# Weights of an MoE and FFN kernel stored on the host in the order of the 1 MB loads, one 8 KB run per partition

## The chip, the cores and the metric

One core of one Trainium2 chip runs the whole program. The metric is the device time in microseconds (us) of one execution. The kernel before took 2174.83 us (median of three runs: 2169.98, 2174.83, 2175.6). The execution that the profiler recorded took 2171.46 us, with a span of 2169.7 us from its first to its last instruction.

## The reference, cut

Two blocks follow each other on 256 tokens of width 1024. Block 1 mixes (gated linear attention beside latent attention) and then runs a routed mixture of 64 experts, two per token. Block 2 has two layers, each a mixer between two dense gated FFNs of hidden width 2816. All arrays are float32.

```python
def hier_moe(u, wg, bg, we, be, w_gate, w_up, w_down):     # w_gate, w_up: 64 x 1024 x 512; w_down: 64 x 512 x 1024
    ...
    def expert_block(args):
        xb, e = args
        hdn = jax.nn.silu(xb @ w_gate[e]) * (xb @ w_up[e])
        return hdn @ w_down[e]
    ...

def swiglu(x, w_gate, w_up, w_down):                       # 1024 x 2816, 1024 x 2816, 2816 x 1024, four times
    return (jax.nn.silu(x @ w_gate) * (x @ w_up)) @ w_down
```

What is computed is the same before and after. The large arrays are these weights: 402.7 MB for the experts (64 of 6 MB), 138 MB for the four FFNs, and some 49 MB for the mixers of both blocks and the memory keys and values.

## The kernel before

All weights come from HBM once, in parts of at most 1 MB, each into one slot of 128 partitions by 2048 floats (8 KB per partition). `load` (L140) takes the next slot of a ring and issues one DMA on SyncE's queue; every weight load has that line. The ring has 17 slots in the expert stage (`a_done` makes it so: three of pool w1, two of w2, five of w4 and seven more) and 3 slots in block 2. A load waits until the last reader of its slot is done. SyncE issues in program order, so later loads wait behind it.

Which bytes of HBM a load takes is set by a rearranged view of the weight:

```python
v = i[src][e].rearrange("(t p q) n -> p t (q n)", p=P, q=2)     # expert gate, up: row 256 t + 2 p + q
v = i["expert_w_down"][e].rearrange("(k p) n -> p k n", p=P)    # expert down: row 128 k + p
v = w[:, c0:c0 + n].rearrange("(k p) n -> p k n", p=P)          # cols_w: 4 or 8 pieces of n columns
```

So one partition of a load is filled from several pieces of HBM. The 1 MB parts of an expert take two runs of 4 KB per partition, and all runs of one part together are 1 MB without a gap. The FFN's gate and up loads (`cols_w`) take four runs of 2 KB per partition, or eight of 1 KB for the first chunk of 256 columns, from rows that lie 11,264 bytes apart; its down loads (`rows_w`) take two of 4 KB. The four w_in chunks of block 1 take four runs of 1856 or 2048 bytes, the memory weights four of 2 KB, `mla_w_qb` two of 3 KB, and the second layer's mixer loads four of 1056 to 2048 bytes or eight of 1 KB.

The program has three stages. Block 1's mixer and router (`phase_a`, to about 180 us) load w_in, w_out and the first experts. The expert stage (`moe`) takes the experts in order. Per expert TensorE multiplies with gate (tile pg from eg) and up (pu from eu), transposes (pt), multiplies with down (pd from ed) and scatters the result back to the tokens (po); every eight experts it gathers the tokens of the next eight (ps). The loads of an expert are issued in the order gate, up, down, two parts each (`load_expert`). In block 2 (from about 1139 us, `ffn` and the mixers) each loaded part is split by ScalarE and VectorE into two halves of its precision (`split`, wh and wl), and TensorE makes three passes per part. `overflow` loads expert weights again where an expert has more than 32 tokens; no load of it is among the DMA issues of the profile.

Of the kernel before, what the change touches and what calls it, by code (L numbers as in the profile page):

```python
# [18 lines left out]
P = 128  # L19
D = 1024  # L20
KD = D // P
# [3 lines left out]
EPS = 1e-6  # L25
LN_EPS = 1e-5
ALL, UPPER, LOWER = (0, 1, 2), (0, 2), (1,)


def _consts():  # L30
# [58 lines left out]
class Kern:  # L89
# [48 lines left out]
    def load(self, shape, src, name, q=None, pool=None):  # L138
        t = self.slot(shape, name, pool=pool)
        (q or self.nc.sync).dma_start(t, src)  # L140
        return t
# [98 lines left out]
    def phase_a(self):  # L240
        nc, tc, i = self.nc, self.tc, self.i
        h = self.h
        w_in = i["w_in"]
# [11 lines left out]
            return sb.tile(shape, F32, tag="t2", bufs=6, name=name)  # L255

        def wcols(c0, n):
            return [self.load([P, 4, n], w_in[512 * u:512 * u + 512, c0:c0 + n].rearrange("(k p) n -> p k n", p=P), "win")
                    for u in range(2)]

        toks = ((0, NM), (NM, P), (NM + P, P))
        met = t4([NM, D], "met")
# [6 lines left out]
        for b in range(2):  # L269
            nc.sync.dma_start(h[:, b, :], i["x"][b * P:(b + 1) * P, :])  # L270
        nc.sync.dma_start(self.cst[0], i["cst0"])
        rest = wcols(0, 464)
        qk = wcols(464, 512)
        wa2 = sb.tile([P, 256], F32, name="wa2")
# [16 lines left out]
        for j in (2, 0, 1):  # L291
            src, n = blocks[j][:2]
# [12 lines left out]
        for j in (0, 2, 1):  # L305
            src, n, c0 = blocks[j]
            for g in range(2):
                p = self.ps()
# [22 lines left out]
        la, e = lae[:, 0], lae[:, 1]  # L331
# [283 lines left out]
        groups = (("kra", 384, 80, 0), ("kv", 256, 128, 0), ("l0", 0, 128, NM), ("l1", 128, 128, NM))  # L615
        zp = {g[0]: self.ps("z") for g in groups}
        rest = [self.split(t, u == 0) for u, t in enumerate(rest)]
        wqb = self.load([P, 2, 768], i["mla_w_qb"].rearrange("(k p) n -> p k n", p=P), "wqb")
        wkvb = self.load([P, 1024], i["mla_w_kvb"], "wkvb")
        for n, c0, w, t0 in groups:  # L620
            zpart(zp[n][:w, t0:NT], rest[0], 0, c0, w, t0, (0, 1))
# [50 lines left out]
        v = self.mp.tile([P, 4, 512], F32, tag="xs", name="v")  # L672
# [32 lines left out]
        for b in range(2):  # L705
            nc.scalar.activation(r_tile()[:, b, :], rp[b], AF.Silu)
        rdone.append(True)

        wo = [self.load([P, 2, D], i["w_out"][256 * u:256 * u + 256, :].rearrange("(k p) n -> p k n", p=P), "wo")
              for u in range(4)]  # L710
        ws = {}
        acc, done = [None, None], False
        for q, b in ((2, 0), (2, 1), (3, 0), (3, 1), (0, 0), (1, 0), (0, 1), (1, 1)):
# [173 lines left out]
    def load_expert(self, e):  # L887
        i = self.i
        out = []
        for n, src in (("eg", "expert_w_gate"), ("eu", "expert_w_up")):  # L890
            v = i[src][e].rearrange("(t p q) n -> p t (q n)", p=P, q=2)
            out.append([self.load([P, 2, D], v[:, 2 * u:2 * u + 2, :], n) for u in range(2)])
        v = i["expert_w_down"][e].rearrange("(k p) n -> p k n", p=P)
        out.append([self.load([P, 2, D], v[:, 2 * u:2 * u + 2, :], "ed") for u in range(2)])
        return out

    def gather(self, e0, parts=((0, 8),)):
# [83 lines left out]
    def overflow(self):  # L981

        nc, tc, i = self.nc, self.tc, self.i
        n = nc.values_load(self.over, min_val=0, max_val=512)
        h = self.h
        mp, mq = self.mp, self.mq
        u2T = mp.tile([P, KD, NX], F32, tag="xg", name="ou")
        wgu = mp.tile([P, 2, D], F32, tag="oh", name="owg")
        wg, wu = (wgu[:, q].rearrange("p (t q n) -> p t q n", t=4, q=2) for q in range(2))
        wd = mp.tile([P, 4 * NT], F32, tag="y", bufs=2, name="owd")[:, :D]  # L990
        s = mq.tile([P, NX], F32, tag="C", bufs=2, name="os")
        gc = mq.tile([P, 2], F32, name="ogc")
        with tc.If(n > 0):
            for b in range(2):
                xv = self.xs[:, b, :].rearrange("p (t x q) -> p t q x", q=2, x=P)
                for k in range(KD):
                    p = self.ps("ot")
                    self.T(p[:, :P], xv[:, k // 2, k % 2, :])
                    nc.vector.tensor_scalar_mul(u2T[:, k, b * P:b * P + P], p[:, :P], self.col("ffn")[:, k:k + 1])
            with tc.For_i(0, 64, 1) as e:  # L1000
                po = [[self.ps("fo") for _ in range(2)] for _ in range(2)]
                nc.sync.dma_start(gc, self.Gov[:, :, bass.ds(e, 1)].rearrange("p b o -> p (b o)"))
                for f in range(4):
                    fs = slice(f * P, f * P + P)
                    for t in range(4):
                        for dst, src in ((wg, "expert_w_gate"), (wu, "expert_w_up")):
                            nc.sync.dma_start(dst[:, t], i[src][bass.ds(e, 1), 256 * t:256 * t + 256, fs].rearrange(
                                "o (p q) n -> p (o q) n", q=2))
                    nc.sync.dma_start(wd, i["expert_w_down"][bass.ds(e, 1), fs, :].rearrange("o p n -> p (o n)"))
                    pp = []  # L1010
                    for wt in (wg, wu):
                        p = self.ps("fg")
                        for k in range(KD):
                            self.mm(p[:, :NX], wt[:, k // 2, k % 2, :], u2T[:, k, :], start=k == 0, stop=k == KD - 1)
                        pp.append(p)
                    nc.scalar.activation(s, pp[0][:, :NX], AF.Silu)
                    nc.vector.tensor_mul(s, s, pp[1][:, :NX])
                    for b in range(2):
                        for nh in range(2):
                            self.mm(po[b][nh], s[:, b * P:b * P + P], wd[:, nh * 512:nh * 512 + 512],  # L1020
                                    start=f == 0, stop=f == 3)
                for b in range(2):
                    for nh in range(2):
                        cs = slice(nh * 512, nh * 512 + 512)
                        nc.vector.scalar_tensor_tensor(h[:, b, cs], po[b][nh], gc[:, b:b + 1], h[:, b, cs],
                                                       ALU.mult, ALU.add)
# [16 lines left out]


    def kv_w(self, l):
        return self.i["w_kv_mem_2"][l].rearrange("(k p) n -> p k n", p=P)

    def load_kv(self, l):
        v = self.kv_w(l)
# [92 lines left out]
        self.mm(out, xh, wl, start=False, stop=False)  # L1142
        self.mm(out, xl, wh, start=False, stop=stop)

    def cols_w(self, w, c0, n):

        v = w[:, c0:c0 + n].rearrange("(k p) n -> p k n", p=P)
        kk = 8 if n <= 256 else 4
        return [lambda k0=k0: self.load([P, kk, n], v[:, k0:k0 + kk, :], "wc") for k0 in range(0, KD, kk)]

    def rows_w(self, w, r0, nk):

        v = w[r0:r0 + nk * P, :].rearrange("(k p) n -> p k n", p=P)
        return [lambda k0=k0: self.load([P, 2, D], v[:, k0:k0 + 2, :], "wr") for k0 in range(0, nk, 2)]

    def xw(self, b, out, w, k0, passes=ALL):

# [84 lines left out]
    def ffn(self, l, j, ln, nxt):  # L1242

        nc, i = self.nc, self.i
        last = nxt is None
        wg, wu, wd = (i[n][l, j] for n in ("ffn_w_gate_2", "ffn_w_up_2", "ffn_w_down_2"))
        g, bt = self.ln_params(l, ln)
        ctx = ExitStack()
        fp = ctx.enter_context(self.tc.tile_pool(name="fp", bufs=1))
        chunks = [(0, 256)] + [(256 + 512 * c, 512) for c in range(5)]  # L1250
        nch = len(chunks)
        nkt = sum(n for _, n in chunks) // P
        acc = [None, None]
# [63 lines left out]
        w = self.split(self.cols_w(wg, *chunks[1])[1]())  # L1317
        for b in range(2):
            gu(1, "g", 1, b, w)
        for c in range(1, nch):  # L1320
            if c > 1:
                for h, x in enumerate(self.cols_w(wg, *chunks[c])):
                    w = self.split(x())
                    for b in range(2):
                        gu(c, "g", h, b, w)
            for h, x in enumerate(self.cols_w(wu, *chunks[c])):
                w = self.split(x(), late=c == 1)
                for b in range(2):
                    gu(c, "u", h, b, w)
            c0, n = chunks[c - 1]  # L1330
            ws = self.rows_w(wd, c0, n // P)
            if c < nch - 1:
                for q, x in enumerate(ws):
                    w = self.split(x())
                    for b in range(2):
                        down(c - 1, q, b, w)
        c = nch - 1
        ws += self.rows_w(wd, chunks[c][0], 4)
        w = [None] * 4
# [491 lines left out]
    AT += _w  # L1831


def prep(inp):

    v = {k: np.asarray(x) for k, x in inp.items()}
    v = {k: x[0] if x.ndim > 2 and x.shape[0] == 1 else x for k, x in v.items()}
    rows = [v[k].reshape(4, P, 2).transpose(0, 2, 1) if k == "ffn_norm" else v[k] for _, k in ROWS]
    rows = np.concatenate([x.reshape(-1, P) for x in rows])
    d = {"cst0": CONSTS[0], "cst1": CONSTS[1], "rows": np.concatenate([rows, np.zeros((P - len(rows), P), rows.dtype)])}  # L1840
    w = v["w_in"]
    d["w_in"] = np.concatenate([w[:, 1552:], w[:, 1536:1552], w[:, :1536]], 1)
    w = v["mla_w_qb"].reshape(256, 4, 192)
    d["mla_w_qb"] = np.concatenate([w[:, :, :P].reshape(256, 512), w[:, :, P:].reshape(256, 256)], 1)
    d["wa2"] = np.zeros((P, 256), v["gla_w_a2"].dtype)
    d["wa2"][64:80], d["wa2"][96] = v["gla_w_a2"], v["gla_b_a"].reshape(-1)
    d["wr"] = np.concatenate([v["router_group_w"], v["router_expert_w"]], 1).reshape(4, P, 144).transpose(1, 0, 2)
    d["br"] = np.concatenate([v["router_group_b"].reshape(1, -1), v["router_expert_b"].reshape(1, -1)], 1)
    d["qk_conv_w_2"] = v["qk_conv_w_2"].reshape(64, 96)
    for k in ("mix_norm", "final_norm"):  # L1850
        d[k] = v[k].reshape(1, D)
    for k, x in v.items():
        if k not in d and not any(k in m for m in MIX) and k not in [m for _, m in ROWS]:
            d[k] = x
    return {k: np.ascontiguousarray(x) for k, x in d.items()}
# [14 lines left out]
```

## Time and profile before

| | us |
|---|---|
| three runs | 2169.98, 2174.83, 2175.6 |
| the profiled execution | 2171.46 |
| its span | 2169.7 |
| TensorE busy | 2003.4 (92% of the span) |
| expert stage, first to last matmul of pg, pu, pd | 178.9 to 1140.1 |
| block 2, from there to the end | about 1030 |
| SyncE's DMA queue: packets, bytes | 195,554, 602.55 MB |

A busy TensorE is not a TensorE at its peak, since matmuls are pipelined and their ends are modelled. The share of the DMA engines is the sum of the times of their packets over 16 engines and the stretch. It passes 100% where consecutive packets of one engine overlap a little, so a stretch with about 102% is one in which no engine rests. A packet here is one run of bytes in HBM that goes to one partition; each load adds 16 packets of 4 bytes (one per engine, which tell that it has landed).

### The profile page before, as it was taken

How to read it: one execution, taken by the hardware profiler on the slowest of the kernel's cores; microseconds unless marked ns; L12 is line 12 of the kernel's file. 1: busy time of each engine (PE TensorE's matmuls, PEld its weight loads, DVE VectorE, ACT ScalarE, POOL GpSimd, SP SyncE). 2: the span in 40 equal slices, each digit the busy share in tenths (PEclk: the TensorE clock that was granted, in tenths of full speed). 3: DMA queues.
4: the chain of work that ended last, by engine and by line, in shares of the span. 5: the costliest groups of instructions: out<-in, count | busy, mean ns of one | idle time of the engine just before them, and what ended most of it. 6: DMA issues, size and time to landing. Idle time of an engine off the chain costs nothing.

```text
span 2169.7 us, 36697 instructions
## 1 busy us (share of the span) xinstructions
PE 2003.4 (92%) x15959; PEld 1402.0 (65%) x15959; DVE 955.4 (44%) x1460; ACT 668.3 (31%) x885; POOL 31.3 (1%) x28
## 2 busy tenths in 40 slices
PE   8989888988889898988889999999999999999998
PEld 7767544534444354444447887888888887888886
DVE  6553322222222222222226555775447455887445
ACT  6423111111111111111114433544434432854332
POOL 3000000000000000000000000000000000000000
PEclk9979999999999999999999999999999999999999
DMA  6448999999999999999996654546555553445551
GB/s 225 175 178 348 411 388 411 413 412 413 411 413 412 412 412 413 411 408 412 408 379 219 229 179 144 204 140 219 185 177 192 181 188 92 163 156 186 183 179 74
DMA packets 195942, 604.96 MB, mean 279 GB/s; under 512 B 9889, under 2 KB 26529, under 8 KB 195778
## 3 DMA queue, kind: packets, MB, share of 16 engines
q1 hardware_dynamic: 195554, 602.55, 73.0%
q8 instruction: 127, 2.08, 0.4%
q14 instruction: 37, 0.30, 0.0%
q10 hardware_dynamic: 224, 0.03, 0.0%
HBM read 601.49 MB, written 1.05 MB: 278 GB/s over the span
## 4 chain that ended last, share of the span: by engine, by line
PE 58%; DMA 23%; DVE 4%; SPq 1%; ACT 1%; issue 1%; DVEq 0%; ACTq 0%
DMA ed<-in_expert_w_down 12%; PE fu L117 11%; PE fg L117 11%; PE fd L117 11%; DMA eu<-in_expert_w_up 10%; PE pd L117 5%; PE po L117 4%; PE cu L117 2%; PE mu L117 2%; PE ps L117 2%; PE pg L117 2%; PE pu L117 2%; PE mo L117 2%; SPq L140 1%; PE ht L114 1%
## 5 line engine op out<-in xcount | busy, mean ns | idle before, releaser
L976 DVE SCALAR_TENSOR_TENSOR h<-po,G,h 128x512 f32<-128x512 f32 x256 | 192.1, 751 | 359.0 <-PE po L117 338.7
L1123 DVE TENSOR_TENSOR wl<-wc,wh 128x2048 fp32r<-128x2048 f32 (+2 forms) x108 | 240.3, 2231 | 181.7 <-ACT wh L1117 181.5
L117 PE MATMUL pd<-ed,hT 128*32 128x512 f32 x1024 | 249.5, 640 | 43.7 <-DMA ed<-in_expert_w_down 32.7
L1117 ACT ACTIVATE wh<-wc 128x2048 fp32r<-128x2048 f32 (+2 forms) x114 | 213.0, 1871 | 232.8 <-PE fu L117 75.5
L117 PE MATMUL po<-y,C 128*128 128x512 f32 x512 | 236.7, 605 | 3.8 <-ACT C L970 3.8
L117 PE MATMUL fd<-wh,hT 128*128 128x512 f32 x704 | 234.3, 400 | 0.0
L117 PE MATMUL fg<-wh,xT 128*128 128x512 f32 (+1 forms) x768 | 222.1, 381 | 5.6 <-DVE xT L1136 4.6
L117 PE MATMUL fu<-wh,xT 128*128 128x512 f32 (+1 forms) x768 | 221.8, 378 | 0.0
L117 PEld LDWEIGHTS po<-y,C 128*128 128x128 f32 x512 | 91.8, 189 | 144.6 <-ACT y L965 72.6
L1123 DVE TENSOR_TENSOR wl<-wr,wh 128x2048 fp32r<-128x2048 f32 x52 | 119.2, 2292 | 132.9 <-ACT wh L1117 131.3
L117 PE MATMUL pu<-eu,xg 128*32 128x128 f32 x4096 | 132.4, 275 | 45.4 <-DMA eu<-in_expert_w_up 44.7
L117 PEld LDWEIGHTS fg<-wh,xT 128*128 128x128 f32 x768 | 136.4, 189 | 36.0 <-DVE xT L1136 6.2
L950 DVE TENSOR_TENSOR hg<-sg,pu 128x128 f32<-128x128 f32 x64 | 18.4, 288 | 313.9 <-PE pu L117 313.9
L117 PEld LDWEIGHTS fu<-wh,xT 128*128 128x128 f32 x768 | 136.9, 190 | 29.1
L117 PEld LDWEIGHTS fd<-wh,hT 128*128 128x128 f32 x704 | 132.2, 188 | 30.5
L117 PEld LDWEIGHTS pu<-eu,xg 128*32 128x32 f32 x4096 | 110.3, 110 | 60.4 <-DMA eu<-in_expert_w_up 48.0
L117 PEld LDWEIGHTS pd<-ed,hT 128*32 128x32 f32 x1024 | 50.9, 114 | 149.9 <-issue 93.4
L117 PE MATMUL fd<-wl,hT 128*128 128x512 f32 x352 | 138.5, 393 | 0.0
L970 ACT COPY C<-pc 128x256 f32<-128x256 f32 x64 | 23.9, 373 | 370.8 <-PE pc L114 370.8
L117 PEld LDWEIGHTS pg<-eg,xg 128*32 128x32 f32 x4096 | 107.8, 110 | 44.3 <-issue 39.7
L117 PE MATMUL fu<-wl,xT 128*128 128x512 f32 (+1 forms) x384 | 135.4, 376 | 0.0
L1117 ACT ACTIVATE wh<-wr 128x2048 fp32r<-128x2048 f32 x52 | 99.6, 1915 | 105.3 <-PE fd L117 56.9
(496 smaller groups left out, 2406.4 us busy)
## 6 DMA issues: line engine op xcount, KB each, us to landing
eg<-in_expert_w_gate SPq DMA_DIRECT2D x128, 1024.0 KB, 18.5
eu<-in_expert_w_up SPq DMA_DIRECT2D x128, 1024.0 KB, 18.4
ed<-in_expert_w_down SPq DMA_DIRECT2D x128, 1024.0 KB, 18.4
wc<-in_ffn_w_gate SPq DMA_DIRECT2D x44, 1024.0 KB, 4.9
wc<-in_ffn_w_up SPq DMA_DIRECT2D x44, 1024.0 KB, 4.9
wr<-in_ffn_w_down SPq DMA_DIRECT2D x44, 1024.0 KB, 4.7
wc<-in_w_in_conv SPq DMA_DIRECT2D x10, 1024.0 KB, 5.1
wr<-in_w_out SPq DMA_DIRECT2D x8, 1024.0 KB, 4.8
```

Of the source, the lines that this page charges most:

```text
L114: self.nc.tensor.transpose(out, in_, self.c("ident", p, p))
L117: self.nc.tensor.matmul(out, lhsT, rhs, start=start, stop=stop, **kw)
L140: (q or self.nc.sync).dma_start(t, src)
L950: nc.vector.tensor_mul(hg, sg, pu[:, :P])
L970: nc.scalar.copy(C, p[:, :NX])
L976: nc.vector.scalar_tensor_tensor(self.h[:, b, cs], p, self.G[:, b, e:e + 1], self.h[:, b, cs], ALU.mult, ALU.add)
L1117: nc.scalar.activation(hi, raw, AF.Copy)
L1123: (nc.gpsimd if gp else nc.vector).tensor_sub(lo, raw, hi.bitcast(F32))
```

## The change

`prep`, which runs in numpy on the host, stores every large weight as an array of 128 rows, one per partition, in which each part that a load takes is 2048 consecutive floats (1856, 1536 or 1056 for narrower chunks). `by_rows` does so for weights that are loaded by rows, `by_chunks` for those that are loaded by chunks of columns. Each load then takes one run per partition, of 8 KB for a 1 MB part. The distance in HBM from one partition's run to the next is now the length of such a row: 16 KB for an expert weight (two parts per weight) and for the memory weights, 32 KB for w_out, 88 KB for the FFN weights. The same bytes land in the same places of the same slots, and the order of the loads stays.

```diff
+FFN = [(0, 256)] + [(256 + 512 * c, 512) for c in range(5)]
...
         def wcols(c0, n):
-            return [self.load([P, 4, n], w_in[512 * u:512 * u + 512, c0:c0 + n].rearrange("(k p) n -> p k n", p=P), "win")
-                    for u in range(2)]
+            return [load() for load in self.cols_w(w_in, c0, n, "win")]
...
-        wqb = self.load([P, 2, 768], i["mla_w_qb"].rearrange("(k p) n -> p k n", p=P), "wqb")
+        wqb = self.load([P, 2, 768], i["mla_w_qb"].rearrange("p (k n) -> p k n", n=768), "wqb")
...
     def load_expert(self, e):
         i = self.i
         out = []
-        for n, src in (("eg", "expert_w_gate"), ("eu", "expert_w_up")):
-            v = i[src][e].rearrange("(t p q) n -> p t (q n)", p=P, q=2)
+        for n, src in (("eg", "expert_w_gate"), ("eu", "expert_w_up"), ("ed", "expert_w_down")):
+            v = i[src][e].rearrange("p (t n) -> p t n", n=D)
             out.append([self.load([P, 2, D], v[:, 2 * u:2 * u + 2, :], n) for u in range(2)])
-        v = i["expert_w_down"][e].rearrange("(k p) n -> p k n", p=P)
-        out.append([self.load([P, 2, D], v[:, 2 * u:2 * u + 2, :], "ed") for u in range(2)])
         return out
...
     def kv_w(self, l):
-        return self.i["w_kv_mem_2"][l].rearrange("(k p) n -> p k n", p=P)
+        return self.i["w_kv_mem_2"][l].rearrange("p (k n) -> p k n", n=512)
...
-    def cols_w(self, w, c0, n):
-
-        v = w[:, c0:c0 + n].rearrange("(k p) n -> p k n", p=P)
+    def cols_w(self, w, c0, n, name="wc"):
+
+        v = w[:, KD * c0:KD * c0 + KD * n].rearrange("p (k n) -> p k n", n=n)
         kk = 8 if n <= 256 else 4
-        return [lambda k0=k0: self.load([P, kk, n], v[:, k0:k0 + kk, :], "wc") for k0 in range(0, KD, kk)]
-
-    def rows_w(self, w, r0, nk):
-
-        v = w[r0:r0 + nk * P, :].rearrange("(k p) n -> p k n", p=P)
-        return [lambda k0=k0: self.load([P, 2, D], v[:, k0:k0 + 2, :], "wr") for k0 in range(0, nk, 2)]
+        return [lambda k0=k0: self.load([P, kk, n], v[:, k0:k0 + kk, :], name) for k0 in range(0, KD, kk)]
+
+    def rows_w(self, w, r0, nk, name="wr"):
+
+        v = w.rearrange("p (k n) -> p k n", n=D)
+        return [lambda k0=k0: self.load([P, 2, D], v[:, k0:k0 + 2, :], name) for k0 in range(r0 // P, r0 // P + nk, 2)]
...
+def by_rows(w, t=1):
+
+    a, k, n = w.shape[:-2], w.shape[-2] // (P * t), w.shape[-1]
+    return np.moveaxis(w.reshape(*a, k, P, t * n), -2, -3).reshape(*a, P, k * t * n)
+
+
+def by_chunks(w, widths):
+
+    at = np.concatenate([[0], np.cumsum(widths)])
+    return np.concatenate([by_rows(w[..., a:b]) for a, b in zip(at, at[1:])], -1)
...
+    for k, t in (("expert_w_gate", 2), ("expert_w_up", 2), ("expert_w_down", 1), ("w_out", 1), ("w_out_2", 1),
+                 ("ffn_w_down_2", 1), ("w_kv_mem_2", 1)):
+        d[k] = by_rows(v[k], t)
+    for k, widths in (("ffn_w_gate_2", [n for _, n in FFN]), ("ffn_w_up_2", [n for _, n in FFN]),
+                      ("w_in_conv_2", [512] * 5), ("w_in_mlstm_2", [384] * 4 + [512, 256, 512, 256, 264])):
+        d[k] = by_chunks(v[k], widths)
```

On SyncE's queue every row keeps its place, and only the shape of the source changes. The piece below is the start of that queue (win are the w_in loads of block 1, cst and vrows constants).

```order
 L271 DMA cst_63<-in_cst 128x608
-L140 DMA win_100<-in_w_in 128x4x464
-L140 DMA win_102<-in_w_in 128x4x464
-L140 DMA win_104<-in_w_in 128x4x512
-L140 DMA win_106<-in_w_in 128x4x512
+L141 DMA win_100<-in_w_in 128x1856
+L141 DMA win_102<-in_w_in 128x1856
+L141 DMA win_104<-in_w_in 128x2048
+L141 DMA win_106<-in_w_in 128x2048
 L278 DMA vrows<-in_rows 128x128
```

Four runs per partition have become one, in the same four loads; all engines have as many instructions as before.

## Rows read from the trace of the kernel before

**Rows 1.** The page's 40 equal slices of the span: DMA share in tenths, rate.
```profile
DMA  6448999999999999999996654546555553445551
GB/s 225 175 178 348 411 388 411 413 412 413 411 413 412 412 412 413 411 408 412 408 379 219 229 179 144 204 140 219 185 177 192 181 188 92 163 156 186 183 179 74
```

**Rows 2.** The page's chain that ended last, by engine and by line.
```profile
PE 58%; DMA 23%; DVE 4%; SPq 1%; ACT 1%; issue 1%; DVEq 0%; ACTq 0%
DMA ed<-in_expert_w_down 12%; PE fu L117 11%; PE fg L117 11%; PE fd L117 11%; DMA eu<-in_expert_w_up 10%; PE pd L117 5%; PE po L117 4%; PE cu L117 2%; PE mu L117 2%; PE ps L117 2%; PE pg L117 2%; PE pu L117 2%; PE mo L117 2%; SPq L140 1%; PE ht L114 1%
```

**Rows 3.** Three stretches: busy time of each engine, clock, DMA share, rate.
```profile
core 0: us, PE busy (x) PEld busy (x) DVE busy (x) ACT busy (x) POOL busy (x), PEclk, DMA share, GB/s
200.00:280.00 80.00, 71.41 (x976) 41.62 (x975) 23.92 (x40) 14.17 (x33) 0.00 (x0) 1.00 0.97 387
280.00:1139.00 859.00, 742.18 (x8926) 385.48 (x8928) 210.27 (x354) 128.90 (x282) 0.00 (x0) 0.97 1.02 410
...
1139.00:2170.00 1031.00, 1008.62 (x4866) 827.91 (x4862) 615.08 (x813) 442.20 (x437) 3.09 (x10) 0.99 0.51 173
```

**Rows 4.** Chain in order of time: start us, us, what; experts paced by TensorE, then by DMA.
```profile
309.58 3.63 PE po L117 x8
...
322.16 3.63 PE po L117 x8
...
340.88 20.08 DMA ed<-in_expert_w_down
```

**Rows 5.** Waits from 340 to 1140 us: engine, line, whom it waited for, total.
```profile
PE pu L117 <- DMA eu<-in_expert_w_up: 44.7, 51, 2.8
...
PE pd L117 <- DMA ed<-in_expert_w_down: 32.7, 52, 2.2
```

**Rows 6.** Rate of the DMA engines in 40 slices of 255 to 290 us.
```profile
GB/s 440 384 421 431 398 426 393 426 389 426 398 403 398 421 403 417 403 421 403 389 262 103 0 9 169 412 426 398 440 412 426 389 403 426 417 417 407 407 426 384
```

**Rows 7.** DMA packets and SyncE's queue (q1), 280 to 1139 us.
```profile
DMA packets 92059, 351.85 MB, mean 410 GB/s; under 512 B 5353, under 2 KB 6055, under 8 KB 91974
...
q1 hardware_dynamic: 91974, 350.57, 101.5%
```

**Rows 8.** DMA packets from 12 to 16 us: w_in, runs of 2 KB.
```profile
DMA packets 818, 1.64 MB, mean 409 GB/s; under 512 B 18, under 2 KB 24, under 8 KB 818
```

**Rows 9.** DMA packets from 600 to 606 us: experts, runs of 4 KB.
```profile
DMA packets 657, 2.52 MB, mean 420 GB/s; under 512 B 42, under 2 KB 42, under 8 KB 657
```

**Rows 10.** DMA packets from 1599.5 to 1601 us: an FFN's first chunk, runs of 1 KB.
```profile
DMA packets 563, 0.58 MB, mean 384 GB/s; under 512 B 0, under 2 KB 563, under 8 KB 563
```

**Rows 11.** DMA packets and SyncE's queue (q1), 500 to 600 us: experts alone.
```profile
DMA packets 10653, 41.20 MB, mean 412 GB/s; under 512 B 621, under 2 KB 621, under 8 KB 10644
...
q1 hardware_dynamic: 10644, 41.06, 102.0%
```

**Rows 12.** DMA issues of the page: tile, count, KB each, median us to landing.
```profile
ed<-in_expert_w_down SPq DMA_DIRECT2D x128, 1024.0 KB, 18.4
wc<-in_ffn_w_gate SPq DMA_DIRECT2D x44, 1024.0 KB, 4.9
...
wr<-in_ffn_w_down SPq DMA_DIRECT2D x44, 1024.0 KB, 4.7
```

**Rows 13.** Chain in order of time, start of block 2: the load that TensorE waits out.
```profile
1166.43 5.22 DMA wc<-in_ffn_w_gate
```

**Rows 14.** DMA queues of the whole program: packets, MB, share.
```profile
q1 hardware_dynamic: 195554, 602.55, 73.0%
q8 instruction: 127, 2.08, 0.4%
q14 instruction: 37, 0.30, 0.0%
```

More of the change, by code (lines that the diff above doesn't have):

```diff
@@ L707, in phase_a @@
         rdone.append(True)
-        wo = [self.load([P, 2, D], i["w_out"][256 * u:256 * u + 256, :].rearrange("(k p) n -> p k n", p=P), "wo")
-              for u in range(4)]
+        wo = [load() for load in self.rows_w(i["w_out"], 0, KD, "wo")]
         ws = {}
@@ L1006, in overflow @@
                         for dst, src in ((wg, "expert_w_gate"), (wu, "expert_w_up")):
-                            nc.sync.dma_start(dst[:, t], i[src][bass.ds(e, 1), 256 * t:256 * t + 256, fs].rearrange(
-                                "o (p q) n -> p (o q) n", q=2))
-                    nc.sync.dma_start(wd, i["expert_w_down"][bass.ds(e, 1), fs, :].rearrange("o p n -> p (o n)"))
+                            nc.sync.dma_start(dst[:, t], i[src][bass.ds(e, 1), :, t * D:t * D + D].rearrange(
+                                "o p (q n) -> p (o q) n", q=2)[:, :, fs])
+                    nc.sync.dma_start(wd, i["expert_w_down"][bass.ds(e, 1), :, f * D:f * D + D].rearrange("o p n -> p (o n)"))
                     pp = []
@@ L1249, in ffn @@
         fp = ctx.enter_context(self.tc.tile_pool(name="fp", bufs=1))
-        chunks = [(0, 256)] + [(256 + 512 * c, 512) for c in range(5)]
+        chunks = FFN
         nch = len(chunks)
@@ L1841, in prep @@
     w = v["w_in"]
-    d["w_in"] = np.concatenate([w[:, 1552:], w[:, 1536:1552], w[:, :1536]], 1)
+    d["w_in"] = by_chunks(np.concatenate([w[:, 1552:], w[:, 1536:1552], w[:, :1536]], 1), (464, 512, 512, 512))
     w = v["mla_w_qb"].reshape(256, 4, 192)
-    d["mla_w_qb"] = np.concatenate([w[:, :, :P].reshape(256, 512), w[:, :, P:].reshape(256, 256)], 1)
+    d["mla_w_qb"] = by_rows(np.concatenate([w[:, :, :P].reshape(256, 512), w[:, :, P:].reshape(256, 256)], 1))
+    for k, t in (("expert_w_gate", 2), ("expert_w_up", 2), ("expert_w_down", 1), ("w_out", 1), ("w_out_2", 1),
[4 more added lines that the diff above has]
+        d[k] = by_chunks(v[k], widths)
     d["wa2"] = np.zeros((P, 256), v["gla_w_a2"].dtype)
```

## The prediction

> **What bounds the kernel now.** I read the 40 slices first: what the DMA engines are doing in each stage. The reader is to see a plateau of about 412 GB/s with all 16 engines occupied through the middle half of the run, and half of that rate or less in block 2 [rows 1]. The stretches give it in numbers: from 280 to 1139 us a DMA share of 1.02 at 410 GB/s, with TensorE busy for 742.18 of 859 us. After 1139 us it is the other way round, with TensorE busy for 1008.62 of 1031 us and a DMA share of 0.51 [rows 3]. The chain that ended last agrees: 23% of the span is DMA, and 22 of these 23 points are loads of expert weights [rows 2]. So two stages with two bounds: the experts wait for HBM loads, block 2 for TensorE.
>
> Where the DMA bound begins matters, since a faster load is worth something only behind that point. Early experts run at TensorE's pace: from one scatter (po) to the next 12.58 us, and the chain first goes through a load at 340.88 us [rows 4]. That is the effect, not the start. The cause lies where the engines last ran dry, with all 17 slots full: at about 274 to 276 us the rate falls to 0 and returns [rows 6]. From there on the stream runs without a rest until the last expert has landed, so its end is that point plus the bytes over the rate. From 200 to 280 us the rate is 387 GB/s and the share 0.97 [rows 3]. There a faster engine would only rest longer, and I cost that part at nothing.
>
> **The change, part by part.** Bytes, loads, their order and every instruction stay. What changes is the number of packets: a 1 MB load had 16 packets of 4 KB for each of the 16 engines (32 of 2 KB, 64 of 1 KB), and has 8 of 8 KB. So the question is what a packet costs beside its bytes. No 8 KB packet of SyncE's queue is in the trace, so I take the cost from stretches in which all engines are full with packets of one size, less the small packets that mark landings:
> - 1 KB: 563 packets in 1.5 us on 16 engines [rows 10], 35.2 per engine, **42.6 ns** each.
> - 2 KB: 818 less 18 in 4 us [rows 8], 50 per engine, **80.0 ns** each.
> - 4 KB: 657 less 42 in 6 us [rows 9], 38.4 per engine, **156.1 ns** each.
>
> The straight line through the outer two has 37.8 ns per KB and 4.8 ns per packet. From neighbours alone I get 2 x 42.6 - 80.0 = 5.2 ns and 2 x 80.0 - 156.1 = 3.9 ns. I take 4.8 ns, and keep 3.9 and 5.2 as the near ends.
>
> The trace shows a rate that still rises with the run, 384, 409 and 420 GB/s at 1, 2 and 4 KB [rows 8 to 10]. The Trainium skill (DMA: Bandwidth & Descriptors, section Specifications) has line rate from 512 bytes on, by which 4 KB and 8 KB runs move equally fast and the change gains nothing; that is rival C below. The rows disagree with it, though by less at each doubling. The same page (section Why small descriptors are slow (HBM only)) puts about 3 cycles on each packet, which at its 850 MHz is an estimate of 3.5 ns; by that the sum below would be 10 us instead of 14, and the time 2163 us.
>
> *Experts, 280 to 1139 us.* SyncE's queue moved 350.57 MB there [rows 7]. Two loads of memory weights and about one of block 2 are among it, some 3 MB. The other 347.5 MB are 84,800 packets of 4 KB, 5,300 per engine. Half of them go: 2,650 x 4.8 ns = **12.7 us** (10.3 to 13.8 by the near ends). The two memory loads lose 24 packets per engine each, 0.2 us, and the first loads of block 2, which land at the end of the stream, 0.3 us. Together 13.2 us, all of it on the path, since no engine rests there. TensorE doesn't take over: of its 117 idle us in the stretch, 77.4 are waits for eu and ed [rows 3, 5], and 13 of them go.
>
> *Before 280 us.* Nothing: the loads wait for slots that TensorE frees, and the w_in loads of the start come before TensorE needs them.
>
> *Block 2.* TensorE covers the loads. Uncovered is the load that a stage begins with, such as the 5.22 us at 1166 us [rows 13]. It has 24 packets fewer per engine, 0.115 us; with four FFNs and two mixers at most 0.7 us, and I take 0.6. That 2 KB and 4 KB loads land after 4.9 and 4.7 us [rows 12] says that no more is to be had. If a load came late, ScalarE's split would be late next, and then TensorE.
>
> *The sum* is 13.2 + 0.6 = 13.8 us, or 0.6%. From the profiled execution's 2171.5 us that gives 2157.7. That execution lies 3.4 us below the median of the three runs, and all four lie between 2170.0 and 2175.6 with a mean of 2173.0. Less 13.8 this is **2159 us**, my forecast for a median. A change of 0.3%, 6.5 us, is about what a measurement of this kernel can tell from none.
>
> The far ends: over the longest run of experts alone a packet of 4 KB takes not 156.1 but (10644 - 621) / 16 = 626 per engine in 100 us, 159.6 ns [rows 11]. So 3.5 ns per packet come from something that the best 6 us lack. If that goes by bytes, it stays, and the sum above holds. If it goes by packets, half of it goes as well. If it is a limit of all engines together that grows as they get faster, it eats the gain.
>
> **The rivals.**
>
> *B, the 3.5 ns go by packets.* Then another 2,650 x 3.5 ns = 9.3 us go, 23.1 in all, and the time is 2150 us. For it: the excess is there with runs of 4 KB and nothing else in the queue. Against it: engines that get in each other's way over memory would do so by the byte, and the 2 KB stretch shows 80.0 ns, which lies on the line without any excess.
>
> *C, the run is not the limit.* Either the rate of all engines together is capped near 412 GB/s when it has to last, or the 8 KB run is cut into two packets on its way. Then only part of block 2's 0.6 us is left, and the time is 2172 to 2173 us. For it: 412 GB/s hardly moves over the whole plateau [rows 1], and the gain from 2 to 4 KB had shrunk to 1% when 2 KB (409) is held against the lasting 412. Against it: 420 GB/s over 6 us, and packets of 16 KB that other queues of this program send undivided (2.08 MB in 127 packets [rows 14]).
>
> *D, the other side: the runs of one load now lie apart.* Before, the 128 x 2 runs of an expert part made 1 MB without a gap. Now 128 runs of 8 KB stand 16 KB apart, and every engine's next run begins at the same place in a 16 KB grid. If such runs meet in the same part of the memory, each packet waits. The forecast has 2 x 159.6 - 4.8 = 314.4 ns for 8 KB, and each ns more costs 2,650 x 1 ns = 2.65 us. The gain is gone at 319.6 ns, and from 322 ns on the kernel is slower by over 0.3%. If the excess, 7 ns per 8 KB now, tripled to 21 ns, the packet would take 328.4 ns: 37 us more, 2196 us. Against it: the w_in loads take rows 8,000 bytes apart and ran at 409 GB/s without excess [rows 8]. For it: that distance is no power of two, and 16 KB is one.
>
> **How the numbers follow.** The forecast has a chance of 0.57, B 0.18, C 0.17, D 0.08. A and B are faster by over 0.3%: 0.75. C is the same: 0.17. D is slower: 0.08. The range runs from 3 us below B to C's lower end, 2147 to 2172 us. It leaves out D, half of C and a tail of B.
>
> **What would show it.** In the profile of the changed kernel: SyncE's queue with about 85,000 packets in place of 195,554 and the same bytes (else the run is cut, C); a plateau of 417 to 419 GB/s in the slices in place of 412 (426 would be B, 412 C, under 410 D); expert loads that land some 0.3 us earlier than after 18.4 us, since as many are in flight; a start of the first expert where it was, and all of the gain between 280 us and the last expert's landing; block 2 as long as now, within 1 us. The forecast is wrong if the plateau keeps its rate, or if block 2 or block 1 gives more than 2 us.

## The result: 22 us less, nearly all of it in the expert stage

The changed kernel takes 2150.53 us (median of four runs, 2148.83 to 2151.05) where the kernel before, with one run more beside it, takes 2172.4 us. The ratio is 0.9901, with a 95% interval of 0.9877 to 0.9924. The forecast of 2159 us was 8.5 us too high. The time lies where the prediction saw rival B, at 2150 us.

The page of the changed kernel, its 40 slices, answers to [rows 1]:

```profile
DMA  6448999999999999999986553545545553445451
GB/s 227 176 181 348 421 394 421 422 420 422 421 422 420 422 422 421 422 422 422 412 353 242 194 188 136 201 162 208 180 176 196 180 183 104 143 158 196 176 188 67
```

The plateau now stands at 420 to 422 GB/s, with all engines occupied as before. It lies between the forecast's 417 to 419 and the 426 that the prediction gave for B. The second half of the run is unchanged in kind.

Its DMA packets and SyncE's queue over the whole program answer to [rows 14], its issues (count, KB each, median us to landing) to [rows 12]:

```profile
DMA packets 85990, 604.96 MB, mean 282 GB/s; under 512 B 9889, under 2 KB 10145, under 8 KB 14914
...
q1 hardware_dynamic: 85602, 602.55, 70.8%
```
```profile
ed<-in_expert_w_down SPq DMA_DIRECT2D x128, 1024.0 KB, 19.8
wc<-in_ffn_w_gate SPq DMA_DIRECT2D x44, 1024.0 KB, 4.6
...
wr<-in_ffn_w_down SPq DMA_DIRECT2D x44, 1024.0 KB, 4.6
```

So 85,602 packets carry the same 602.55 MB: the run of 8 KB leaves as one packet, and the half of rival C in which it is cut is gone. The loads of block 2 land after 4.6 us in place of 4.7 and 4.9. Those of the experts land later, after 19.8 us in place of 18.4, which the prediction had the other way round.

The stretches answer to [rows 3], cut where this kernel's stages end (columns as there):

```profile
200.00:280.00 80.00, 69.68 (x972) 40.84 (x971) 24.31 (x40) 14.19 (x33) 0.00 (x0) 1.00 0.97 397
280.00:1117.00 837.00, 735.92 (x8924) 384.38 (x8924) 209.23 (x353) 128.96 (x281) 0.00 (x0) 0.98 1.01 419
1117.00:2147.00 1030.00, 1008.47 (x4867) 828.07 (x4866) 615.04 (x813) 442.66 (x437) 3.10 (x10) 1.00 0.48 173
```

Before 280 us the rate is 397 GB/s in place of 387, but two more profiles of the changed kernel have 378 and 382 there, so nothing can be told of that stretch. Then it is 419 GB/s in place of 410. The last stretch takes 1030 us in place of 1031. Where the stages end is shown more sharply by the first matmul on a gate matrix (pg) and the last on a down matrix (pd): count, duration in ns, first and last start in us. Before:

```profile
L117 PE MATMUL pg<-eg,xg x4096: 272/273/298, 178.9 to 1130.9; 128*32 128x128 f32 x196
```
```profile
L117 PE MATMUL pd<-ed,hT x1024: 589/592/1063, 184.6 to 1140.1; 128*32 128x512 f32 x171
```

and after:

```profile
L118 PE MATMUL pg<-eg,xg x4096: 272/273/298, 177.2 to 1110.5; 128*32 128x128 f32 x196
```
```profile
L118 PE MATMUL pd<-ed,hT x1024: 589/592/1063, 182.9 to 1118.4; 128*32 128x512 f32 x171
```

From the first pg to the last pd it was 961.2 us and is 941.2 us. In two more profiles of the changed kernel it was 944.4 and 943.8. The first pg came 1.7 us earlier here, but 0.2 and 0.6 us earlier in those two. From the last pd to the end it was 1029.6 us and is 1028.7 (1029.0 and 1027.5 in the other two). So 17 to 20 us went in the expert stage, at most 2 us in block 1 and 0.6 to 2.1 us in block 2. What block 2 shows can't be told from nothing: a kernel with block 2 as it was (the experts alone, below) has 1028.2 us there.

The 100 us that give the length of a packet answer to [rows 11]:

```profile
DMA packets 5779, 42.15 MB, mean 422 GB/s; under 512 B 643, under 2 KB 643, under 8 KB 643
...
q1 hardware_dynamic: 5769, 41.99, 100.6%
```

5769 less 643 packets on 16 engines are 320.4 per engine, **312.1 ns** for 8 KB. Two packets of 4 KB took 319.2 ns. That is 7.1 ns less where the forecast took off 4.8 and rival B 8.3.

### The profile page after: what moved, and what is told of

Same layout as the page of the kernel before. It is cut to its first block, busy times and chain, and to the rows that moved or that the text cites. A ratio compares the mean times of both kernels' runs of the same rounds, so it can differ in the third digit from the quotient of the medians.

```text
span 2147.1 us, 36697 instructions
## 1 busy us (share of the span) xinstructions
PE 1995.2 (93%) x15959; PEld 1399.5 (65%) x15959; DVE 955.6 (45%) x1460; ACT 668.9 (31%) x885; POOL 31.3 (1%) x28
## 3 DMA queue, kind: packets, MB, share of 16 engines
q1 hardware_dynamic: 85602, 602.55, 70.8%
## 4 chain that ended last, share of the span: by engine, by line
PE 62%; DMA 30%; DVE 5%; ACT 2%; issue 1%; SPq 0%; DVEq 0%; ACTq 0%
DMA ed<-in_expert_w_down 14%; PE fu L118 12%; PE fg L118 11%; PE fd L118 11%; DMA eu<-in_expert_w_up 8%; DMA eg<-in_expert_w_gate 7%; PE ps L118 4%; PE po L118 4%; PE pd L118 4%; PE cu L118 3%; PE mu L118 2%; PE pg L118 2%; PE mo L118 2%; PE pu L118 1%; PE wo L118 1%; PE ht L115 1%
## 5 line engine op out<-in xcount | busy, mean ns | idle before, releaser
L1120 DVE TENSOR_TENSOR wl<-wc,wh 128x2048 fp32r<-128x2048 f32 (+2 forms) x108 | 240.3, 2231 | 178.1 <-ACT wh L1114 177.9
L947 DVE TENSOR_TENSOR hg<-sg,pu 128x128 f32<-128x128 f32 x64 | 18.5, 288 | 300.8 <-PE pu L118 300.8
## 6 DMA issues: line engine op xcount, KB each, us to landing
eg<-in_expert_w_gate SPq DMA_DIRECT2D x128, 1024.0 KB, 19.8
eu<-in_expert_w_up SPq DMA_DIRECT2D x128, 1024.0 KB, 19.8
ed<-in_expert_w_down SPq DMA_DIRECT2D x128, 1024.0 KB, 19.8
```

The costliest lines, as they stand in the source:

```text
L947: nc.vector.tensor_mul(hg, sg, pu[:, :P])
L1120: (nc.gpsimd if gp else nc.vector).tensor_sub(lo, raw, hi.bitcast(F32))
```

## The experiments

Thirteen runs of the changed kernel, four beside the prediction and nine with the experiments, lie between 2142.9 and 2153.9 us. Medians of single experiments that differ by less than 3 us are therefore told apart only by their intervals, if at all. Two theories stood at the start: P, that the number of packets alone makes the gain, and L, that what exceeds 4.8 ns per packet comes from the new distances in HBM.

### The changed kernel again

> The changed kernel itself, beside the others on one chip, as their yardstick. Both theories: about 22 us below the kernel before (ratio 0.990), a rate of 422 GB/s from 500 to 600 us, 312 ns for a packet of 8 KB there.

2150.43 us, ratio 0.9909 (0.9896 to 0.9921), 311.8 ns per packet of 8 KB from 500 to 600 us. So these two measurements of it agree within 0.1 us; a third, further below, gave 2146.75 us.

### 8 KB runs, parts without gaps

```diff
-            v = i[src][e].rearrange("p (t n) -> p t n", n=D)
-            out.append([self.load([P, 2, D], v[:, 2 * u:2 * u + 2, :], n) for u in range(2)])
+            v = i[src][e].rearrange("u p (t n) -> u p t n", n=D)
+            out.append([self.load([P, 2, D], v[u], n) for u in range(2)])
...
+        if k.startswith("expert"):
+            d[k] = np.moveaxis(d[k].reshape(64, P, 2, 2 * D), 2, 1)
```

> The changed kernel with each 1 MB part of an expert without gaps in HBM again: still one 8 KB run per partition, but the next partition's run begins 8 KB further instead of 16 KB. If the gain comes from the packets alone (theory P): as the changed kernel within 2 us, 422 GB/s from 500 to 600 us. If the part of the gain beyond 4.8 ns per packet, some 2.3 ns per 8 KB or 6 us, comes from the new distances (theory L): 418 GB/s there, and 6 us slower than the changed kernel, about 2157 us where that has 2151.

2150.68 us, ratio 0.9903 (0.9888 to 0.9919). Its DMA packets from 500 to 600 us:

```profile
DMA packets 5773, 42.14 MB, mean 421 GB/s; under 512 B 638, under 2 KB 638, under 8 KB 638
...
q1 hardware_dynamic: 5763, 41.99, 100.6%
```

(5763 - 638) / 16 is 320.3 per engine, 312.2 ns. Theory L asked for 314.4 ns and 6 us more, and falls. Whether the runs of a load touch or lie 16 KB apart makes no difference here.

### 4 KB runs, partitions 16 KB apart

```diff
-            v = i[src][e].rearrange("p (t n) -> p t n", n=D)
-            out.append([self.load([P, 2, D], v[:, 2 * u:2 * u + 2, :], n) for u in range(2)])
+            v = i[src][e].rearrange("p (k u n) -> p u k n", u=2, n=D)
+            out.append([self.load([P, 2, D], v[:, u], n) for u in range(2)])
...
+        if k.startswith("expert"):
+            d[k] = np.moveaxis(d[k].reshape(64, P, 2, 2, 1024), 2, 3).reshape(64, P, 4 * D)
```

> The changed kernel with every expert part in two runs of 4 KB per partition again, 8 KB apart, partitions still 16 KB apart; all other weights as in the changed kernel. Theory P: 4 KB packets take 159.6 ns again, 412 GB/s from 500 to 600 us, and only the gain of the other weights stays, 2 to 3 us below the kernel before. Theory L: 4.7 / 2 = 2.3 ns of excess per packet instead of 3.5, so 158.4 ns, 414 GB/s, and about 6 us more of gain, 8 to 9 us below the kernel before.

2172.4 us, ratio 1.0007 (0.9997 to 1.0017). From 500 to 600 us:

```profile
DMA packets 10653, 41.19 MB, mean 412 GB/s; under 512 B 625, under 2 KB 625, under 8 KB 10643
...
q1 hardware_dynamic: 10643, 41.04, 101.9%
```

(10643 - 625) / 16 is 626.1 per engine, 159.7 ns, as in the kernel before (159.6). The packets' size alone brings the whole time back. The 2 to 3 us that the other weights were to keep are not there either: the interval leaves them 0.7 us at most.

### 2 KB runs

```diff
-            v = i[src][e].rearrange("p (t n) -> p t n", n=D)
-            out.append([self.load([P, 2, D], v[:, 2 * u:2 * u + 2, :], n) for u in range(2)])
+            v = i[src][e].rearrange("p (k u n) -> p u k n", u=2, n=512)
+            out.append([self.load([P, 4, 512], v[:, u], n).rearrange("p (t q) n -> p t (q n)", q=2) for u in range(2)])
...
+        if k.startswith("expert"):
+            d[k] = np.moveaxis(d[k].reshape(64, P, 2, 4, 512), 2, 3).reshape(64, P, 4 * D)
```

> The changed kernel with every expert part in four runs of 2 KB per partition, 4 KB apart. If a packet has the same fixed cost over a long run that 4 KB and 8 KB show there, 2 x 159.7 - 312.1 = 7.3 ns, a packet of 2 KB takes 83.5 ns and the rate is 393 GB/s: 5,300 x (2 x 83.5 - 159.7) = 39 us above the run with 4 KB, about 2211 us where that has 2172. If it is 4.8 ns and the rest of the excess goes by bytes, 82.0 ns, 400 GB/s, 23 us above, about 2195 us. If fewer loads in flight cost something of their own (rival: the queue holds so many packets that 7.2 loads of 4 KB were in flight, so 3.7 of 2 KB), slower than 2211 us. Loads land after 2.7 x 3.7 = 10 us in that case, after 21 us if eight are in flight.

2210.82 us, ratio 1.0187 (1.0161 to 1.0214). From 500 to 600 us:

```profile
DMA packets 19725, 39.28 MB, mean 393 GB/s; under 512 B 599, under 2 KB 599, under 8 KB 19717
...
q1 hardware_dynamic: 19717, 39.16, 104.4%
```

(19717 - 599) / 16 is 1194.9 per engine, 83.7 ns. The first case had 83.5 ns and 2211 us, the second 82.0 ns and 2195 us. So over 100 us a packet costs as much beside its bytes at 2 KB as between 4 and 8 KB. With 83.7, 159.7 and 312.1 ns the line through the outer two has 38.1 ns per KB and **7.6 ns per packet**, and gives 159.8 ns at 4 KB. The landing times were wrong: 14.1 us, between the 10 and the 21 expected. The number of loads in flight cost nothing of its own that this run could show.

### Only the experts, and only the rest

The kernel before with `load_expert` and the experts' `by_rows` of the change, and the changed kernel without them.

> The kernel before with only the expert weights in the new order. All theories: first expert matmul at 178.9 us as before, the expert stage 19 to 20 us shorter, block 2 as before, in all 19 to 20 us below the kernel before and 2 to 3 us above the changed kernel. If block 1 and block 2 owe their shorter times to something else than their own loads, this run has them too and reaches the changed kernel's time.

> The changed kernel with the experts as before: only the other weights in the new order. All theories: expert stage as in the kernel before, 412 GB/s from 500 to 600 us. If the 1.7 us by which the first expert began earlier in the changed kernel's first profile come from the shorter w_in loads, the first expert matmul is at about 177.2 us and the time 2 to 3 us below the kernel before. If they are chance (other profiles with the new order had 177.9 to 178.7), it is at 177 to 179 us and the time within 1.5 us of the kernel before.

The experts alone: 2153.97 us, ratio 0.9921 (0.9908 to 0.9935), first expert matmul at 178.7 us, 943.6 us from the first pg to the last pd. The rest alone: 2168.79 us, ratio 0.999 (0.9975 to 1.0005), first expert matmul at 177.9 us, 412 GB/s from 500 to 600 us. So the experts give 17 us (14 to 20) of the 22. The rest gives between nothing and 5 us by this run, and at most 0.7 us by the run with 4 KB runs, which has it too. The experts alone and the changed kernel on the same chip (0.9896 to 0.9921) have intervals that overlap, so the 22 and the 17 us do not contradict each other. With first matmuls between 177.1 and 178.7 us for the new w_in layout, and 178.7 us for the old one in the experts' run, the first matmul alone doesn't tell what w_in gives; the granted clock beside it does (under Block 1, below).

### Runs 1 MB apart

```diff
+    def expert_w(self, src):
+        return self.i[src].rearrange("p (e m) -> e p m", e=64)
...
-            v = i[src][e].rearrange("p (t n) -> p t n", n=D)
+            v = self.expert_w(src)[e].rearrange("p (t n) -> p t n", n=D)
...
+        if k.startswith("expert"):
+            d[k] = np.moveaxis(d[k], 0, 1).reshape(P, 64 * 4 * D)
```

> The changed kernel with all 64 experts of one weight in one row per partition, so that the runs of a load lie 1 MB apart instead of 16 KB. If distances don't matter for a load of 8 KB runs: as the changed kernel, 422 GB/s, 2150 us. If rival D's mechanism exists at larger powers of two: a lower rate in the whole expert stage, and each per cent of rate costs 8.5 us; at 330 GB/s the time would be about 2380 us.

2157.91 us, ratio 0.9938 (0.9916 to 0.9959), so some 7 us behind the changed kernel. From 500 to 600 us a packet takes 311.9 ns, (5767 - 637) / 16 per engine. The stretches from 900 and from 1000 us on:

```profile
900.00:1000.00 100.00, 86.47 (x1073) 41.83 (x1066) 26.11 (x45) 12.74 (x28) 0.00 (x0) 0.97 1.01 422
1000.00:1080.00 80.00, 67.92 (x801) 35.43 (x800) 15.90 (x28) 12.54 (x28) 0.00 (x0) 0.94 1.01 390
```

The plateau is untouched until 1000 us, and then the rate falls to 390 GB/s, though no engine rests. From 1000 to 1040 us it is 390 GB/s as well, where the changed kernel's three profiles have 421 and 422. Why only the last experts suffer is open; one profile shows it. The Trainium skill (DMA: Bandwidth & Descriptors, section Latency and other measured facts) reports copies between HBM tensors at 207 GB/s with the partitions' rows 512 KiB apart, 164 at 2 MiB and 103 at 4 MiB. For loads of 8 KB runs 1 MB apart the plateau of this run shows no such loss.

### Fewer slots

```diff
-        w3 = [self.one.enter_context(self.tc.tile_pool(name=f"w3{q}", bufs=1, reuse_waits="tile")) for q in range(7)]
+        w3 = [self.one.enter_context(self.tc.tile_pool(name=f"w3{q}", bufs=1, reuse_waits="tile")) for q in range(1)]
```

> The changed kernel with 11 slots instead of 17 in the expert stage, so fewer loads in flight with the same packets of 8 KB. If the packets alone set the rate: 422 GB/s from 500 to 600 us, loads landing after about 12 us, time within 3 us of the changed kernel. If part of the gain came from having 8 loads in flight instead of 7.2, the rate falls to 418 GB/s or less and the time rises by 8 us or more. If TensorE's pauses now empty the queue, the DMA share falls below 1 and the time rises by more than that.

2165.69 us, ratio 0.9981 (0.9966 to 0.9995), with 311.9 ns per packet and a landing time of 19.7 us, as with 17 slots. So as many loads were in flight, the run says nothing on their number, and the time was missed by 12 us. The reason is to be seen ahead of the stage, from 50 to 180 us, in this kernel and in the changed one (columns as in [rows 3]):

```profile
50.00:180.00 130.00, 117.56 (x761) 95.20 (x760) 71.94 (x179) 47.57 (x74) 9.03 (x2) 0.95 0.45 163
```
```profile
50.00:180.00 130.00, 118.50 (x704) 96.82 (x706) 70.78 (x176) 45.67 (x70) 9.02 (x2) 0.89 0.51 194
```

With six slots fewer, 163 GB/s flow in place of 194 while block 1 computes, 4.0 MB less in 130 us. What isn't loaded there has to be loaded in a stage that is bound by its loads. From the first pg (171.7 us) to the last pd (1129.2 us) that stage takes 957.5 us here, 13 to 16 us more than in the three profiles of the changed kernel; six slots of 1 MB at 2.50 us (8 x 312.1 ns) are 15 us. So by one profile each slot filled ahead was worth about its whole load. The stage also began 5.5 to 7 us earlier, along with a higher granted clock of TensorE from 50 to 180 us, 0.95 in place of 0.89; why it is higher is open. So the profiled execution, 2160.52 us and one of the shortest of ten, lies only 7 to 12 us above those of the changed kernel, while the medians lie 15 us apart.

### Without the branch

```diff
-            if e == 7:
-                self.overflow()
-            elif e == ne - 4:
+            if e == ne - 4:
```

> The changed kernel without the branch after the eighth expert (it leaves out what is done for experts with more than 32 tokens, which these inputs don't have). If the DMA engines run dry near 270 us because SyncE lets all loads in flight land before the branch, the rate no longer falls to 0 there, and the end comes earlier by about the hole, some 2 to 4 us: about 2147 us where the changed kernel has 2150.5. If they run dry because all slots are full, the hole stays and the time is the changed kernel's within 1.5 us.

2148.51 us, ratio 0.9888 (0.9869 to 0.9907). The hole is gone; from 200 to 280 us:

```profile
200.00:280.00 80.00, 71.62 (x982) 42.77 (x981) 25.99 (x43) 14.65 (x34) 0.00 (x0) 1.00 1.00 415
```

A DMA share of 1.00 and 415 GB/s, where the changed kernel has 0.97 and 397 (0.93 with 378 and 382 in its other two profiles). So the engines ran dry because of the branch, not because slots were full. SyncE's waits in the kernel before, 240 to 282 us, say the same (who waited for whom, us in total, times, longest): L993 is the branch's line.

```profile
SPq L993 <- SPq L993: 17.7, 7, 2.6
```

Beside the three medians of the changed kernel, 2150.5, 2150.4 and 2146.8 us, the gain in time is unclear: 2 us against the first two, none against the third, which was taken on the same chip.

### The last memory loads in the ring

```diff
-        return [self.load([P, 4, 512], v[:, 4 * u:4 * u + 4, :], "wkv", pool=self.w4) for u in range(2)]
+        return [self.load([P, 4, 512], v[:, 4 * u:4 * u + 4, :], "wkv") for u in range(2)]
```

> The changed kernel with the last two memory loads in the next slots of the ring instead of slots of pool w4, which TensorE still reads when SyncE comes to them. If the half rate from about 1066 to 1077 us comes from SyncE waiting there for a slot with the experts' loads behind it, the rate stays near 420 GB/s there, the experts end about 5 us earlier, and the time falls by 3 to 5 us, to about 2147 us. If the experts' end is set by something else by then, the time is the changed kernel's within 1.5 us.

> The changed kernel again, as the yardstick of the other two on this chip: 2150.5 us within 1.5, holes at about 270 and 1070 us.

2151.28 us, ratio 0.9905 (0.9889 to 0.9922), and the changed kernel beside it 2146.75 us (2142.89 to 2151.39), ratio 0.9877 (0.9858 to 0.9896). Of all thirteen runs of the changed kernel its two short ones (2142.9 and 2143.2 us) have the highest granted clock over the whole run, 0.985 and 0.986, where the others have 0.978 to 0.983. From 1050 to 1090 us, first this kernel, then the changed one on the same chip:

```profile
1050.00:1090.00 40.00, 35.35 (x357) 15.66 (x346) 9.71 (x17) 6.37 (x13) 0.00 (x0) 0.96 1.00 411
```
```profile
1050.00:1090.00 40.00, 34.73 (x370) 15.89 (x371) 8.50 (x15) 6.35 (x13) 0.00 (x0) 0.96 0.93 379
```

The hole closes (411 in place of 379 GB/s, no engine rests), so its cause was the wait for a slot. The time doesn't follow. From the first pg to the last pd it is 941.3 us where the changed kernel's profiles have 941.2 to 944.4, which can't be told apart. So this version beats nothing, though a hole of about 3 us was shut; where that went is open.

## Why the prediction was right in kind and short in size

**The bound was read rightly.** Expert loads set the pace and block 2 did not care: the stage gave 17 to 20 us, block 2 nothing that can be told from none, and TensorE did not take over.

**The term that came out too small is the cost of a packet beside its bytes.** The prediction took 4.8 ns from three stretches of 1.5 to 6 us [rows 8 to 10]. Over 100 us it is 7.6 ns. The prediction had seen the difference, 3.5 ns between the best 6 us and the long stretch [rows 9, 11], and let it go by bytes. The runs show that it goes by packets: above the short stretches' 80.0 and 156.1 ns the long ones have 3.7 ns at 2 KB and 3.6 ns at 4 KB. At 8 KB the excess over the forecast's own 2 x 156.1 - 4.8 = 307.4 ns is 4.7 ns. Twice the bytes don't double it. That was rival B's case, with a chance of 0.18.

The "best 6 us" of the experts were nothing but the best. Sixteen stretches of 6 us, one after the other from 500 us on, have 156.1 to 162.4 ns per packet in the kernel before, with a mean of 159.7, and 307.7 to 316.8 ns in the changed kernel, with a mean of 312.1. The shortest and one of the longest before, from 518 and from 572 us on:

```profile
DMA packets 651, 2.52 MB, mean 420 GB/s; under 512 B 36, under 2 KB 36, under 8 KB 651
...
q1 hardware_dynamic: 651, 2.52, 102.6%
```
```profile
DMA packets 636, 2.44 MB, mean 406 GB/s; under 512 B 44, under 2 KB 44, under 8 KB 635
...
q1 hardware_dynamic: 635, 2.42, 101.2%
```

The lowest such stretches of each size, 80.4 ns with runs of 2 KB, 156.1 with 4 KB and 307.7 with 8 KB, give 4.6 ns per packet again, the means 7.6. So 4.8 ns is the price in the best few microseconds, and the stage pays the mean. What in the hardware makes the difference is open.

The sum with the measured price: 2,650 x 7.1 ns = 18.8 us for the experts, and with the forecast's own 0.5 us for the other loads of the stage, 19.3 us. The forecast had 13.2, and the profiles show 17 to 20. With the 0.6 us for block 2 this is 19.9 us, and from the prediction's 2173.0 us it gives 2153 us. No run shows the 0.5 and the 0.6 us by themselves. That the time lies within 1 us of rival B's 2150 us is luck in part, as B took off 8.3 ns per pair of packets and 7.1 were measured; the interval of the result, 17 to 27 us, holds both sums.

**The Trainium skill's price was too low as well.** Its 3 cycles per packet (DMA: Bandwidth & Descriptors, section Why small descriptors are slow (HBM only)), an estimate of 3.5 ns, would have given 2163 us. That estimate leaves out the 32 bytes of descriptor that the same section adds to each operation. The measurement decides: 7.6 ns over 100 us of loads from HBM.

**The point where the stream starts was right, its reason wrong.** The prediction had all 17 slots full at about 274 us. The branch of `overflow` stands there, and SyncE lets every load in flight land before it. That the stage's end hangs on what was loaded by the time the stream starts fits the run with 11 slots.

**The landing time was wrong.** It was to fall by 0.3 us, "since as many are in flight", and rose by 1.4. The duration of the DMA instructions of eg on SyncE (ns, smallest, median, largest; then first and last start) shows why, before, after, and with runs of 2 KB:

```profile
L140 SPq DMA_DIRECT2D eg<-in_expert_w_gate x128: 367/2292/4848, 88.6 to 1110.7; - x128
```
```profile
L141 SPq DMA_DIRECT2D eg<-in_expert_w_gate x128: 327/328/749, 86.9 to 1087.6; - x128
```
```profile
L141 SPq DMA_DIRECT2D eg<-in_expert_w_gate x128: 540/2498/5007, 89.5 to 1158.6; - x128
```

Before, an issue held SyncE for 2.3 us in the median, now for 0.33. What holds it now is another wait, for an earlier load to land. From 200 to 1040 us SyncE's longest waits in total were these, before and after (columns as for the wait at the branch):

```profile
SPq L140 <- PE po L117: 144.0, 68, 4.8
```
```profile
SPq L141 <- DMA ed<-in_expert_w_down: 223.8, 105, 3.5
```

With eg and eu such waits for a landing are 659 us in the changed kernel; in the kernel before they are 19 us. At 2.55, 2.50 and 2.68 us per load, landing times of 18.5, 19.8 and 14.1 us are 7.2, 7.9 and 5.3 loads in flight, an estimate (the landing time over the time per load).

**Rival D** did not happen: the packet's time is the same with runs that touch, 16 KB apart or, on the plateau until 1000 us, 1 MB apart. **Rival C**'s cap near 412 GB/s does not exist, since 422 lasts as long.

**Block 1** got nothing in the forecast, and the runs leave it next to nothing. The first expert came 0.2 to 1.7 us earlier in the profiles, but its start goes with TensorE's granted clock. From 50 to 70 us, in the kernel before and in the changed one (columns as in [rows 3]):

```profile
50.00:70.00 20.00, 15.77 (x79) 12.90 (x77) 9.97 (x15) 5.47 (x9) 4.50 (x1) 0.83 0.48 158
```
```profile
50.00:70.00 20.00, 15.77 (x84) 12.82 (x83) 9.89 (x14) 6.47 (x10) 4.50 (x1) 0.91 0.43 155
```

In slices of 1 us the clock is at its lower level there (0.50 of full speed, 1.2 in place of 2.4 GHz) for about 7 us before and 3 to 4 us after, both times behind a pause of 4.2 us in which TensorE waited for ScalarE. Where profiles agree in this clock (0.83) and in that from 110 to 140 us (0.60), the first expert begins at 178.7 and 178.9 us with the old order of w_in (the experts alone, the kernel before) and at 178.5 to 178.7 us with the new one (the changed kernel again, 4 KB runs, the memory loads in the ring). So at most 0.4 us are left for the order of w_in. Why the clock differs is open.

## What to carry to other kernels

Where a stage is bound by loads, halve the number of packets and look at what a packet costs over a long stretch: here 7.6 ns beside 38.1 ns per KB, so 2 KB, 4 KB and 8 KB runs give 393, 412 and 422 GB/s. Weights can be stored by the host in the order in which they are loaded at no cost to the kernel, and how far the runs lie apart made no difference here up to 16 KB; at 1 MB the last experts were slower, and the kernel by 7 us. Take such a price from the longest stretch that the stage itself offers, not from the best few microseconds.

## What the runs showed of the hardware that was not expected

Fewer loads were in flight when they were made of more packets: 7.9 loads of 8 packets per engine, 7.2 of 16, 5.3 of 32 (estimates from the landing times). What limits them is not the same. With 16 and 32 packets the issue itself holds SyncE, for 2.3 and 2.5 us in the median. With 8 it holds SyncE for 0.33 us, and SyncE waits for earlier loads to land instead. Here that cost no time that a run could show, but SyncE issues in program order, so its other DMAs wait behind such an issue. And a branch on SyncE let all loads in flight land first, 17.7 us of waiting, after which the DMA engines had nothing to do until the next load had started.
